# A DeepNorm decoder layer on one core: plain products for six contraction tiles of each down projection, the bias table in the mixer, memory queries by seven block products

## The chip, the core and the metric

One core of a Trainium2 chip runs the whole layer in one launch. The metric is the device time of that core in microseconds. Before the change three runs took 1260.83, 1260.99 and 1263.0 us (median 1260.99).

The engines named below: TensorE (PE in the rows) multiplies matrices and transposes, its weight loads are listed as PEld; VectorE (DVE), ScalarE (ACT) and GpSimd (POOL) work elementwise; SyncE (SP) and GpSimd issue DMAs.

## The reference

One layer for 512 tokens of width 1024, in four post-normalised parts:

```
h = LN1(alpha*h + 0.5*SwiGLU_1(h))            # w1, w3: 1024x2816, w2: 2816x1024
h = LN2(alpha*h + W_o[g_mla*Up_mla(MLA(h)) + g_diff*Up_diff(Diff(h))])
h = LN3(alpha*h + MemCrossAttn(h, mem))       # 4 heads of 256, 256 memory rows
h = LN4(alpha*h + 0.5*SwiGLU_2(h))
```

`SwiGLU(h) = (silu(h w1) * (h w3)) w2`. The mixer (second part) has eight latent-attention heads and four differential heads; the logits of the latter get a relative bias, looked up in a table of 32 buckets. The memory attention is `q = h w_q`, `k, v = mem w_kv`, softmax over the 256 memory rows, and an output projection `w_o`.

## The kernel before

All products keep close to full precision: each operand is split into a high and a low part in a rounded format, and a product is three matrix instructions, high x high, high x low and low x high (`mm3`). So every loaded weight tile [128, 1024] passes ScalarE or VectorE for the high part (a cast) and VectorE for the low part (a subtraction), and so does every activation tile.

**Seven products for eight.** Most of the feed-forward networks run by a scheme that multiplies 2x2 block matrices with seven block products, on sums and differences of the blocks. `products` (line 569) does it for a pair of hidden tiles: weight blocks come from a `Unit` (line 485), which loads four blocks of [128, 1024], adds some of them on VectorE and splits seven tiles; the sums of h are made once (`sums_of_h`, line 540) from the raw transposed h (`h_raw`). Each of the seven is 24 matrix instructions with 256 columns; results are combined on the way out. `down7` (line 722) does the same for four tiles of the hidden dimension in the down projection: seven products of 12 instructions with 512 columns, on sums of the gated activations (`Forms`, line 681).

**A feed-forward network** (`ffn`, line 639) has 22 hidden tiles. Tiles 0 and 1 are plain. Then come five groups: two calls of `seven`, two hidden tiles each, and one `down7` for four tiles (0 to 19 in all). Groups 0 to 3 add their results to an accumulator in DRAM by accumulating DMAs of GpSimd (after ScalarE has copied them from PSUM); group 4 adds on VectorE onto `res.acc`, which is loaded back at the start of that group's second `seven`. The last sum (`Residual.add`, line 454) takes tiles 20 and 21 plainly, by token tile (four of 128) and half of the columns: 6 matrix instructions of 512 columns for each, whose result VectorE adds. After the second half of a token tile its layer norm follows (`Norm`, line 392), then eight transposes, from which `hT`, the split transposed h, is written.

**The mixer** (line 1159) begins with four gate projections in two halves of 256 tokens (`project_halves`, line 343): the first half needs two normalised token tiles. The feed-forward network after the third norm begins in the same way.

**The table** (`bias_table`, line 811, with `lam_calc`, line 829) is made in the first network, from a mark at 200 us of the planner's clock: a 33-row one-hot matrix times the bias rows, two products in four passes, stored to DRAM; the differential heads read it later.

**Memory** (`memory`, line 1359): keys (8 weight tiles, no use of h), then the queries plainly, one projection of 24 instructions with 512 columns for each of 8 tiles, then values in two halves (48 instructions each). `mem_heads` (line 1289) runs beside this: for each pair of heads four score tiles, softmax, transposes, and the outputs; the second pair starts when the first pair's outputs are issued. The output projection adds in two steps of four contraction tiles, the second with norm 3.

**What sets the order.** A planner (`Issue`, line 52) runs all these as generators. Each has a rank, lower first; a generator may wait for a mark, a time on the planner's clock. Elementwise work is issued when the planner's clock reaches its start, weight splits with a delay. A scheduler behind it assigns buffers and may move instructions forward; each engine then executes its own list in order. Weights come through three raw and five split buffers (`Weights`, line 269): a tile is fetched when an earlier one is done. Most other tiles share 20 buffers of 4 KB per partition (`slot`).

Of the kernel before, what the change touches and what calls it, by code (L numbers as in the profile page):

```python
# [18 lines left out]
P = 128  # L19
# [175 lines left out]
def layer(ctx: ExitStack, tc: tile.TileContext, a: dict, out: bass.AP):  # L195
# [197 lines left out]
    class Norm:  # L393
# [223 lines left out]
    def plan_ffn(n, w1, w3, w2):  # L617
        for f in range(2):
            W.plan(f"w1_{n}_{f}", w1[f])
            W.plan(f"w3_{n}_{f}", w3[f])  # L620

        def up(p):
            return Unit(f"wp{n}_{p}", [[w[2 * p + i % 2][:, i // 2 * 512:i // 2 * 512 + 512] for w in (w1, w3)] for i in range(4)], ORDER)

        def down(g):
            rows = [w2[f * P:(f + 2) * P].rearrange("(f p) c -> p f c", p=P) for f in (4 * g, 4 * g + 2)]
            return Unit(f"wd{n}_{g}", [rows[i // 2][:, :, i % 2 * 512:i % 2 * 512 + 512] for i in range(4)], DOWN)

        units = []
        for g in range(5):  # L630
            units += [up(2 * g + 1), up(2 * g + 2), down(g)]
        for u, v in zip(units, units[1:]):
            u.after = v
        for u in units:
            u.plan()
        for f in (20, 21):
            W.plan(f"w2_{n}_{f}", w2[f * P:(f + 1) * P])

    def ffn(n, src, ready=None):
        res = Residual(n, src)  # L640
        gT, sums, raw = {}, {}, {}
# [24 lines left out]
        def seven(p, late=()):  # L666

            gated = raw[p] = slot(f"G{n}_{p}", F32)

            def out(c, half, ps, sign):  # L670
                dst = gated[:, c, 256 * half:256 * half + 256]
                act.activation(dst, ps[:, :256], AF.Silu, scale=sign)
                dve.scalar_tensor_tensor(dst, ps[:, 256:], 0.5 * sign, dst, op0=ALU.mult, op1=ALU.mult)
                if half and p == 10:
                    f = 2 * p + c
                    gT[f] = slot(f"g{n}_{f}")
                    split(gT[f][:, 0], gT[f][:, 1], gated[:, c])

            return products(f"wp{n}_{p}", sums, out, dict(late))
# [36 lines left out]
        def load_old():  # L716
            for h in range(2):
                for c in range(2):
                    t = old[h, c] = slot(f"old{n}_{h}_{c}", F32)
                    sp.dma_start(t, rows(src[256 * h:256 * h + 256, c * 512:c * 512 + 512]))  # L720

        def down7(g, forms):

            def product(pss, i, first):
# [5 lines left out]
                W.done(f"wd{n}_{g}_{i}")  # L730

            def add(pss, h, c, sign, new=False):
                if g == 4:
                    for t in range(2):
                        dst = res.acc[2 * h + t][:, c * 512:c * 512 + 512]
                        dve.tensor_tensor(dst, dst, pss[t], op=ALU.add if sign > 0 else ALU.subtract)
                elif g == 0 and new:
                    st = old.pop((h, c))
                    for t in range(2):
                        dve.scalar_tensor_tensor(st[:, t], st[:, t], ALPHA, pss[t], op0=ALU.mult, op1=ALU.add if sign > 0 else ALU.subtract)  # L740
                    sp.dma_start(rows(acc[h, c]), st)
                else:
                    st = slot(f"st{n}_{g}_{h}_{c}", F32)
                    for t in range(2):
                        act.activation(st[:, t], pss[t], AF.Copy, scale=sign)
                    pool.dma_start(rows(acc[h, c]), st, accum_op=ALU.add)

            x = [bank(f"dx{n}_{g}_{t}") for t in range(2)]
            product(x, 1, True)
# [45 lines left out]
                    sp.dma_start(res.acc[t][:, c * 512:c * 512 + 512], acc[t // 2, c][t % 2 * P:t % 2 * P + P])  # L795

        load_old()
        for g in range(5):
            yield from seven(2 * g + 1)
            forms = Forms(g)  # L800
            late = {3: lambda: forms.make(1), 2: lambda: forms.make(2), 4: lambda: forms.make(5)}
            if g == 4:
                late[1] = load_acc
            yield from seven(2 * g + 2, late)
            yield from down7(g, forms)
        yield from res.add(lambda i, t: hl_of(gT[20 + i], slice(t * P, (t + 1) * P)), [f"w2_{n}_{f}" for f in (20, 21)], False, True)


    bias_dram = dram.tile([8, 32 * REL], F32, name="bias_dram")
# [1 line left out]
    def bias_table():  # L811
        rel = const.tile([33, 8], F32, name="rel")
        nc.vector.memset(rel[32:33], NEG)
        sp.dma_start(rel[0:32], a["rel_bias"])
        hot = arena.tile([33, REL], F32, tag="slot", name="hot")
        sp.dma_start(hot, a["onehot"])
        rows = arena.tile([8, REL], F32, tag="slot", name="rows")
        for c in range(2):
            ps = bank(f"rel{c}")
            matmul(ps[:8, :320], rel, hot[:, c * 320:(c + 1) * 320], True, True)  # L820
            dve.tensor_scalar(rows[:, c * 320:(c + 1) * 320], ps[:8, :320], -1.0, None, op0=ALU.mult)
            drop(ps)
        sp.dma_start(bias_dram.rearrange("h (p m) -> h p m", p=32), rows.unsqueeze(1).broadcast_to([8, 32, REL]))


    neglam = const.tile([P, 1], F32, name="neglam")
    gd = const.tile([P, 1], F32, name="gd")

    def lam_calc():
        room = slot("lam", F32, [P, 1024])  # L830
# [328 lines left out]
    def mixer():  # L1159
# [104 lines left out]
    def out_proj(n, w, src, xT, sizes):  # L1264
        res = Residual(n, src)
        k0 = 0
        for m in sizes:
            if n == 3 and k0 + m == KT:
# [7 lines left out]
    def plan_mem():  # L1276
        for j in range(KT):
            W.plan(f"mem_wk{j}", a["mem_wk"][j])
        for j in range(KT):
            W.plan(f"mem_wq{j}", a["mem_w_q"][j])  # L1280
        for c in range(2):
            for q in range(4):
                W.plan(f"mem_wv{c}_{q}", a["mem_wv"][c][:, q * D:(q + 1) * D])
        for k in range(KT):
            W.plan(f"mem_w_o{k}", a["mem_w_o"][k * P:(k + 1) * P])

# [72 lines left out]
    def memory():  # L1359
        def mk(k, toks):  # L1360
            return hl_of(memT[k // 2], slice((k % 2) * 256 + toks.start, (k % 2) * 256 + toks.stop))

        kk, q, vv, oT = [], [], [[None, None], [None, None]], [None] * KT
        for j in range(KT):
            w = W.take(f"mem_wk{j}")
            if j % 2 == 0:
                ps = bank(f"mk{j}")
            dst = ps[:, (j % 2) * 256:(j % 2) * 256 + 256]
            for k in range(KT):
                mm3(dst, hl_of(w, slice(k * P, (k + 1) * P)), mk(k, slice(0, 256)), k == 0, k == KT - 1)  # L1370
            W.done(f"mem_wk{j}")
            if j % 2:
                kk.append(slot(f"mk{j}"))
                split(kk[-1][:, 0], kk[-1][:, 1], ps)
                drop(ps)
            yield
        for t in range(NT):
            yield h_ready[2, t]
        issue.spawn(mem_heads(kk, q, vv, oT), 1)
        for j in range(KT):  # L1380
            ps = yield from project(f"mq{j}", W.take(f"mem_wq{j}"))
            W.done(f"mem_wq{j}")
            t = slot(f"mq{j}")
            split(t[:, 0], t[:, 1], ps, scale=MEM_SCALE)
            drop(ps)
            q.append(t)
            if j % 4 == 3:
                issue.set(mem_q[j // 4], *q)
            yield
        for c in range(2):  # L1390
# [8 lines left out]
            for b in range(2):  # L1399
# [2 lines left out]
                drop(pss[b])  # L1402
                vv[c][b] = v
            issue.set(mem_v[c], *vv[c])
        yield mem_out
        yield from out_proj(3, "mem_w_o", h_dram[1], oT, (4, 4))


    def tables():
        mark = Mark()  # L1410
        mark.floor = 200000.0
        yield mark
        consts()
        bias_table()
        lam_calc()

    def main():
        first_loads()
# [97 lines left out]
```

## Time and profile before

| | before |
|---|---|
| median of three runs | 1260.99 us |
| profiled execution, its own time | 1261.45 us |
| its span, first to last instruction | 1259.70 us |
| mean granted TensorE clock | 0.988 |
| TensorE busy | 1214.5 us, 96% |
| VectorE busy | 1019.4 us, 81% |
| ScalarE busy | 551.0 us, 44% |

Busy time of TensorE contains the pipelined ends of its matrix instructions; the time that a group of them takes is read as the distance from its start to the start of the next. [...]

### The profile page before, as it was taken

To read this page: it belongs to the slowest core of one execution; us is meant where nothing else is said; L and a number is where in the kernel's file an instruction comes from. 1 tells how busy PE (TensorE), PEld (TensorE's weight loads), DVE (VectorE), ACT (ScalarE), POOL (GpSimd) and SP (SyncE) were. 2 spreads that over 40 slices of the span, in tenths; PEclk is the share of its full clock that TensorE was granted. 3 is DMA by queue.
4 is the path that set the end of the run, shared out by engine and by line. 5 is a ranking of instruction groups with operands and counts; after the bars stand their busy time and mean duration, and the time that the engine had idled before them with its cause. 6 is when DMAs were issued, how large, how long until landed. Compare 5 with 4: busy or idle time off the path is not lost. (4 is left out here: it accounts for less than half of the span.)

```text
span 1259.7 us, 19354 instructions
## 1 busy us (share of the span) xinstructions
PE 1214.5 (96%) x7530; PEld 1080.1 (86%) x7530; DVE 1019.4 (81%) x1590; ACT 551.0 (44%) x970; POOL 105.5 (8%) x101
## 2 busy tenths in 40 slices
PE   7999998999979999999999999999999999999995
PEld 5989897889869987877778889888899898999994
DVE  8999989789981799666665695555799999999998
ACT  5343635254432477434441244342453445445451
POOL 0001111111010000000000000000010102130300
PEclk9999999899979999999999999999999999999998
DMA  9749596869231321242233436244493667795941
GB/s 328 220 130 270 114 255 140 201 131 287 73 134 55 124 65 34 64 138 84 84 101 100 150 137 214 72 129 151 162 295 97 173 195 185 184 236 140 254 140 67
DMA packets 86591, 192.52 MB, mean 153 GB/s; under 512 B 7875, under 2 KB 9667, under 8 KB 86500
## 3 DMA queue, kind: packets, MB, share of 16 engines
q1 hardware_dynamic: 68004, 155.64, 37.1%
q0 software_dynamic: 18496, 35.66, 16.1%
q8 instruction: 59, 0.97, 0.3%
q14 instruction: 32, 0.26, 0.1%
HBM read 152.86 MB, written 38.40 MB: 152 GB/s over the span
## 5 line engine op out<-in xcount | busy, mean ns | idle before, releaser
L178 DVE TENSOR_TENSOR wp_hl<-wp_b,wp_hl 128x1024 fp32r<-128x1024 f32 x140 | 168.2, 1220 | 12.9 <-ACT wp_hl L178 10.6
L260 PE MATMUL pzwp<-S,wp_hl 128*128 128x256 f32 x960 | 124.2, 286 | 0.3 <-DVE S L178 0.3
L260 PE MATMUL pxwp<-S,wp_hl 128*128 128x256 f32 x960 | 122.6, 283 | 1.6 <-ACT p_wp L178 1.6
L260 PEld LDWEIGHTS pzwp<-S,wp_hl 128*128 128x128 f32 x960 | 120.0, 194 | 1.6 <-issue 1.1
L260 PE MATMUL pxwp<-hT,wp_hl 128*128 128x256 f32 x960 | 119.9, 281 | 1.3 <-ACT wp_hl L178 1.3
L260 PEld LDWEIGHTS pxwp<-hT,wp_hl 128*128 128x128 f32 x960 | 117.3, 188 | 4.2 <-ACT wp_hl L178 1.7
L260 PEld LDWEIGHTS pxwp<-S,wp_hl 128*128 128x128 f32 x960 | 118.3, 191 | 2.0 <-ACT p_wp L178 2.0
L178 ACT CAST wp_hl<-wp_b 128x1024 fp32r<-128x1024 f32 x75 | 78.7, 1051 | 93.3 <-PE pxwp L260 51.6
L260 PE MATMUL dx<-wd_hl,A 128*128 128x512 f32 x480 | 117.4, 391 | 1.6 <-DVE acc L178 1.2
L260 PEld LDWEIGHTS dx<-wd_hl,A 128*128 128x128 f32 x480 | 88.2, 188 | 21.2 <-issue 3.2
L178 DVE TENSOR_TENSOR wp_b<-wp_b,wp_b 128x1024 f32<-128x1024 f32 x80 | 97.4, 1219 | 0.6
L178 DVE TENSOR_TENSOR wd_hl<-wd_b,wd_hl 128x1024 fp32r<-128x1024 f32 x70 | 85.2, 1220 | 9.2 <-ACT wd_hl L178 9.2
L170 POOL DMA_DIRECT2D acc<-st x48 | 59.5, 1561 | 379.7 <-ACT st L178 205.1
L178 ACT CAST wd_hl<-wd_b 128x1024 fp32r<-128x1024 f32 x52 | 54.5, 1052 | 54.5 <-PE pxwp L260 24.9
L260 PE MATMUL pywp<-hT,wp_hl 128*128 128x256 f32 x480 | 60.6, 280 | 0.3 <-ACT wp_hl L178 0.3
L260 PE MATMUL dz<-wd_hl,A 128*128 128x512 f32 x240 | 59.2, 392 | 0.5 <-ACT st L178 0.3
L260 PEld LDWEIGHTS pywp<-hT,wp_hl 128*128 128x128 f32 x480 | 58.3, 188 | 0.5 <-ACT wp_hl L178 0.5
L260 PE MATMUL pw<-hT,w_hl 128*128 128x256 f32 (+1 forms) x288 | 49.8, 333 | 6.8 <-DVE w_hl L178 5.0
L260 PEld LDWEIGHTS dz<-wd_hl,A 128*128 128x128 f32 x240 | 44.5, 188 | 11.0 <-ACT st L178 1.1
L260 PEld LDWEIGHTS pw<-hT,w_hl 128*128 128x128 f32 x288 | 42.2, 194 | 13.5 <-ACT hT L178 7.2
L178 DVE CAST wp_hl<-wp_b 128x1024 fp32r<-128x1024 f32 x65 | 46.1, 710 | 7.4 <-PE pzwp L260 6.1
L260 PE MATMUL pgd<-hT,w_gd_hl 128*128 128x512 f32 x192 | 47.5, 400 | 0.0
(333 smaller groups left out, 2300.9 us busy)
## 6 DMA issues: line engine op xcount, KB each, us to landing
wp_b<-in_ffn_w SPq DMA_DIRECT2D x160, 256.0 KB, 6.9
wd_b<-in_ffn_w SPq DMA_DIRECT2D x50, 512.0 KB, 10.0
acc<-st POOLq DMA_DIRECT2D x48, 512.0 KB, 9.9
wd_b<-in_ffn_w POOLq DMA_DIRECT2D x20, 512.0 KB, 12.9
h_dram<-acc SPq DMA_DIRECT2D x12, 512.0 KB, 3.1
w_raw<-in_ffn_w SPq DMA_DIRECT2D x11, 512.0 KB, 5.3
w_gm_raw<-in_w_gate SPq DMA_DIRECT2D x8, 512.0 KB, 3.5
acc<-old SPq DMA_DIRECT2D x8, 512.0 KB, 3.7
```

The lines of the kernel that those rows point to most:

```text
L170: return (name, 1000.0, 4000.0, lambda: getattr(engine, op)(*args, **kw)), args[:1], list(args)
L178: return (name, ns, 1500.0 if name == "sync" else 0.0, lambda: getattr(engine, op)(*args, **kw)), outs, ins
L260: issue.pe(lambda: nc.tensor.matmul(ps, w, x, start=start, stop=stop, skip_group_check=again), ps, w, x)
```

## The change

Three parts.

1. Down projections: the fifth group keeps its two calls of `seven` but has no `down7`. Hidden tiles 16 and 17 go through a new plain `down` between the two calls, added to DRAM through `stage`; tiles 18 to 21 form the last sum, now four contraction tiles. `res.acc` is loaded during the sixth product of the last `seven`. The gated activations of tiles 20 and 21 are split by halves of the tokens as they come (`ends`).
2. The table is started as a generator of rank 8 in the mixer, when all four token tiles of norm 1 are transposed; it issues its loads, waits 15 us on the planner's clock, then does its products and the lambda computation (in a work tile).
3. Memory queries go through `Unit` and `products`, two blocks of four query tiles; the sums are made after norm 2 from copies of the raw transposed h. The first half of the values comes before the queries, the second half after them, and `mem_heads` starts after the queries.

```diff
@@ Norm.turn
-                if n == 3:
+                if n in (2, 3):
@@ plan_ffn
-        for g in range(5):
+        for g in range(4):
             units += [up(2 * g + 1), up(2 * g + 2), down(g)]
+        units += [up(9), up(10)]
...
             u.plan()
+            if u is units[-2]:
+                for f in (16, 17):
+                    W.plan(f"w2_{n}_{f}", w2[f * P:(f + 1) * P])
-        for f in (20, 21):
+        for f in range(18, 22):
@@ seven, out
-                if half and p == 10:
+                if p == 10:
+                    if half not in ends:
+                        ends[half] = slot(f"ge{n}_{half}").rearrange("p c (i t) -> p c i t", i=2)
+                    split(ends[half][:, c, 0], ends[half][:, c, 1], dst)
+                elif half and p > 7:
@@ ffn
+        def stage(pss, h, c, sign):
+            st = slot(f"st{n}_{h}_{c}", F32)
+            for t in range(2):
+                act.activation(st[:, t], pss[t], AF.Copy, scale=sign)
+            pool.dma_start(rows(acc[h, c]), st, accum_op=ALU.add)
+
+        def down(fs):
+            keys = [f"w2_{n}_{f}" for f in fs]
+            ws = [W.take(key) for key in keys]
+            for h in range(2):
+                for c in range(2):
+                    pss = [bank(f"ds{n}_{h}_{c}_{t}") for t in range(2)]
+                    for t in range(2):
+                        for w, f in zip(ws, fs):
+                            toks = slice((2 * h + t) * P, (2 * h + t + 1) * P)
+                            mm3(pss[t], hl_of(gT[f], toks), hl_of(w, slice(c * 512, c * 512 + 512)), f == fs[0], f == fs[-1])
...
+                    stage(pss, h, c, 1.0)
...
-        for g in range(5):
+        for g in range(4):
...
+        yield from seven(9)
+        yield from down(range(16, 18))
+        yield from seven(10, {2: load_acc})
+        fs = range(18, NF)
...
+        yield from res.add(part, [f"w2_{n}_{f}" for f in fs], False, True)
@@ bias_table
         sp.dma_start(hot, a["onehot"])
+        yield later(15000.0)
...
+        lam_calc()
@@ mixer
+        issue.spawn(bias_table(), 8, ready[NT - 1])
@@ plan_mem
+        values(0)
+        units = [Unit(f"mem_wq{u}", [[a["mem_w_q"][4 * u + 2 * w + i % 2][:, i // 2 * 512:i // 2 * 512 + 512] for w in range(2)]
+                                     for i in range(4)], ORDER) for u in range(2)]
+        units[0].after = units[1]
...
+        values(1)
@@ memory
+        issue.spawn(summing(), 0)
...
+        yield from values(0)
+        yield summed
+        for u in range(2):
+            def out(c, half, ps, sign, u=u):
+                for w in range(2):
+                    j = 4 * u + 2 * w + c
+                    if not half:
+                        q[j] = slot(f"mq{j}")
+                    toks = slice(256 * half, 256 * half + 256)
+                    split(q[j][:, 0, toks], q[j][:, 1, toks], ps[:, 256 * w:256 * w + 256], scale=sign * MEM_SCALE)
+            yield from products(f"mem_wq{u}", sums, out)
+        issue.spawn(mem_heads(kk, q, vv, oT), 1)
...
+        yield from values(1)
@@ tables
-        bias_table()
-        lam_calc()
```

## Rows read from the trace of the kernel before

**Rows 1.** The page, first part: busy us (share of the span), number of instructions.

```profile
PE 1214.5 (96%) x7530; PEld 1080.1 (86%) x7530; DVE 1019.4 (81%) x1590; ACT 551.0 (44%) x970; POOL 105.5 (8%) x101
```

**Rows 2.** Waits of TensorE: total us, times, longest us.

```profile
PE trh L269 <- DVE acc L178: 9.3, 2, 6.0
...
PE rel L260 <- DMA hot<-in_onehot: 4.4, 1, 4.4
```

**Rows 3.** Windows: stretch, busy us of each engine, clock, DMA share, GB/s.

```profile
364.00:368.00 4.00, 0.00 (x0) 0.00 (x0) 4.00 (x7) 1.80 (x4) 0.93 (x2) 0.50 0.27 63
...
220.00:224.00 4.00, 2.19 (x4) 0.36 (x4) 0.97 (x3) 0.20 (x1) 3.47 (x3) 0.50 0.54 76
```

**Rows 4.** Timeline, first network: start, duration, engine, operation, count, idle before.

```profile
152.96 3.02 PE L260 MATMUL pxwp<-hT,wp_hl 128*128 128x256 f32 x24
...
212.03 3.01 PE L260 MATMUL pxwp<-hT,wp_hl 128*128 128x256 f32 x24
...
215.51 0.37 SPq L178 DMA_DIRECT2D hot<-in_onehot  x1
...
221.81 2.30 PE L260 MATMUL rel<-hot,rel 33*8 33x320 f32 x4 [4.41 <-DMA hot<-in_onehot]
...
224.04 5.13 PE L260 MATMUL pzwp<-S,wp_hl 128*128 128x256 f32 x24
...
283.94 3.02 PE L260 MATMUL pxwp<-hT,wp_hl 128*128 128x256 f32 x24
```

**Rows 5.** Chain that ended last, last network: start, us to the next piece, what.

```profile
1116.69 2.85 PE pxwp L260 x24
...
1122.41 2.88 PE pxwp L260 x24
...
1175.75 2.85 PE pxwp L260 x24
```

**Rows 6.** Timeline at the third norm.

```profile
906.25 5.71 PE L260 MATMUL res_mem_w_o<-mem_w_o_hl,moT 128*128 128x512 f32 x24
...
912.58 7.29 PE L260 MATMUL pw<-hT,w_hl 128*128 128x256 f32 x60
```

**Rows 7.** Timeline at the end of the last network.

```profile
1238.18 9.23 PE L260 MATMUL res_w<-w_hl,g 128*128 128x512 f32 x40
...
1250.88 0.68 DVE L178 SCALAR_TENSOR_TENSOR acc<-acc,res_w 128x512 f32<-128x512 f32 x1
```

**Rows 8.** Timeline at the end of the first network.

```profile
359.23 3.68 PE L269 MATMUL trh<-ident,acc 128*128 128x128 f32 x16 [3.33 <-DVE acc L178]
...
372.13 22.77 PE L260 MATMUL pw_gm<-hT,w_gm_hl 128*128 128x256 f32 x192
...
394.74 9.53 PE L260 MATMUL cq<-w_cq_hl,hT 128*128 128x384 f32 x53
```

**Rows 9.** Groups by form, 773 to 867: count, busy us, mean ns, idle before.

```profile
L260 PE MATMUL mq<-hT,mem_wq_hl 128*128 128x512 f32 x192 | 46.1, 398 | 0.0
...
L178 DVE TENSOR_TENSOR mem_wq_hl<-mem_wq_raw,mem_wq_hl 128x1024 fp32r<-128x1024 f32 x5 | 6.1, 1226 | 12.7 <-ACT mem_wq_hl L178 12.7
```

**Rows 10.** Windows: before the queries, and blocks of the last network.

```profile
760.00:780.00 20.00, 20.00 (x141) 18.69 (x140) 11.34 (x12) 9.66 (x12) 0.00 (x0) 1.00 0.74 244
...
1060.00:1080.00 20.00, 20.00 (x170) 20.00 (x170) 17.01 (x20) 7.37 (x12) 6.23 (x5) 1.00 0.99 244
```

**Rows 11.** Timeline, scores and softmax of the first pair of heads.

```profile
798.52 5.92 PE L260 MATMUL mx<-mk,mq 128*128 128x256 f32 x48
...
804.29 0.50 ACT L178 ACTIVATE me<-me,mrs 128x256 f32<-128x256 f32 x1
...
805.92 0.52 ACT L178 ACTIVATE me<-me,mrs 128x256 f32<-128x256 f32 x1
...
807.48 0.51 ACT L178 ACTIVATE me<-me,mrs 128x256 f32<-128x256 f32 x1
```

**Rows 12.** The page, DMA issues: count, KB each, median us to landing.

```profile
wp_b<-in_ffn_w SPq DMA_DIRECT2D x160, 256.0 KB, 6.9
```

More of the change, by code (lines that the diff above doesn't have):

```diff
@@ L640, in ffn @@
         res = Residual(n, src)
-        gT, sums, raw = {}, {}, {}
+        gT, ends, sums, raw = {}, {}, {}, {}
         acc = {(h, c): dram.tile([256, 512], F32, name=f"acc{n}_{h}_{c}") for h in range(2) for c in range(2)}
@@ L720, in load_old @@
                     sp.dma_start(t, rows(src[256 * h:256 * h + 256, c * 512:c * 512 + 512]))
+        def stage(pss, h, c, sign):
[13 more added lines that the diff above has]
+                            mm3(pss[t], hl_of(gT[f], toks), hl_of(w, slice(c * 512, c * 512 + 512)), f == fs[0], f == fs[-1])
+                    if h and c:
+                        for key in keys:
+                            W.done(key)
+                    stage(pss, h, c, 1.0)
+                    drop(*pss)
+                    yield
         def down7(g, forms):
@@ L732, in add @@
             def add(pss, h, c, sign, new=False):
[L733 to L737, printed above, removed]
+                if g == 0 and new:
                     st = old.pop((h, c))
@@ L742, in add @@
                 else:
[L743 to L746, printed above, removed]
+                    stage(pss, h, c, sign)
             x = [bank(f"dx{n}_{g}_{t}") for t in range(2)]
@@ L797, in ffn, with part @@
         load_old()
-        for g in range(5):
+        for g in range(4):
             yield from seven(2 * g + 1)
             forms = Forms(g)
[L801 to L804, printed above, removed]
+            yield from seven(2 * g + 2, {3: lambda: forms.make(1), 2: lambda: forms.make(2), 4: lambda: forms.make(5)})
             yield from down7(g, forms)
-        yield from res.add(lambda i, t: hl_of(gT[20 + i], slice(t * P, (t + 1) * P)), [f"w2_{n}_{f}" for f in (20, 21)], False, True)
+        yield from seven(9)
+        yield from down(range(16, 18))
+        yield from seven(10, {2: load_acc})
+        fs = range(18, NF)
+        def part(i, t):
+            if i < 2:
+                return hl_of(gT[fs[i]], slice(t * P, (t + 1) * P))
+            return [ends[t // 2][:, i - 2, j, t % 2 * P:t % 2 * P + P] for j in (0, 1)]
+        yield from res.add(part, [f"w2_{n}_{f}" for f in fs], False, True)
     bias_dram = dram.tile([8, 32 * REL], F32, name="bias_dram")
@@ L823, in bias_table, with later @@
         sp.dma_start(bias_dram.rearrange("h (p m) -> h p m", p=32), rows.unsqueeze(1).broadcast_to([8, 32, REL]))
+        lam_calc()
+        yield
+    def later(ns):
+        mark = Mark()
+        mark.floor = issue.clock + ns
+        return mark
     neglam = const.tile([P, 1], F32, name="neglam")
@@ L829, in lam_calc @@
     def lam_calc():
-        room = slot("lam", F32, [P, 1024])
+        room = wk("lam")
         lam = room[:, :256].rearrange("p (a b) -> p a b", a=4)
@@ L1267, in out_proj @@
         for m in sizes:
-            if n == 3 and k0 + m == KT:
+            if k0 + m == KT:
                 h_raw.extend(slot(f"hraw{j}", F32) for j in range(4))
@@ L1278, in plan_mem, with values @@
             W.plan(f"mem_wk{j}", a["mem_wk"][j])
-        for j in range(KT):
-            W.plan(f"mem_wq{j}", a["mem_w_q"][j])
-        for c in range(2):
+        def values(c):
             for q in range(4):
                 W.plan(f"mem_wv{c}_{q}", a["mem_wv"][c][:, q * D:(q + 1) * D])
+        values(0)
+        units = [Unit(f"mem_wq{u}", [[a["mem_w_q"][4 * u + 2 * w + i % 2][:, i // 2 * 512:i // 2 * 512 + 512] for w in range(2)]
+                                     for i in range(4)], ORDER) for u in range(2)]
+        units[0].after = units[1]
+        for u in units:
+            u.plan()
+        values(1)
         for k in range(KT):
@@ L1361, in mk, with summing, values @@
             return hl_of(memT[k // 2], slice((k % 2) * 256 + toks.start, (k % 2) * 256 + toks.stop))
[L1363 to L1390, printed above, removed]
+        kk, q, vv, oT = [], [None] * KT, [[None, None], [None, None]], [None] * KT
+        sums, summed = {}, Mark()
+        def summing():
+            for t in range(NT):
+                yield h_ready[2, t]
+            mark = sums_of_h(2, sums)
+            summed.floor, summed.ops = mark.floor, mark.ops
+        def values(c):
             pss = [bank(f"mv{c}_{b}") for b in range(2)]
@@ L1404, in memory @@
             issue.set(mem_v[c], *vv[c])
+        issue.spawn(summing(), 0)
+        for j in range(KT):
+            w = W.take(f"mem_wk{j}")
+            if j % 2 == 0:
+                ps = bank(f"mk{j}")
+            dst = ps[:, (j % 2) * 256:(j % 2) * 256 + 256]
+            for k in range(KT):
+                mm3(dst, hl_of(w, slice(k * P, (k + 1) * P)), mk(k, slice(0, 256)), k == 0, k == KT - 1)
+            W.done(f"mem_wk{j}")
+            if j % 2:
+                kk.append(slot(f"mk{j}"))
+                split(kk[-1][:, 0], kk[-1][:, 1], ps)
+                drop(ps)
+            yield
+        yield from values(0)
[10 more added lines that the diff above has]
+        issue.spawn(mem_heads(kk, q, vv, oT), 1)
+        for hp in range(2):
+            issue.set(mem_q[hp], *q)
+        yield from values(1)
         yield mem_out
@@ L1409, in tables @@
     def tables():
-        mark = Mark()
-        mark.floor = 200000.0
-        yield mark
+        yield later(200000.0)
         consts()
-        bias_table()
-        lam_calc()
     def main():
```

## The prediction

> **What bounds the kernel now.** The page's first part comes first: TensorE is busy for 96% of the span and VectorE for 81% [rows 1]. So a stage costs what TensorE executes in it, plus the places where it stands still. Those are listed by the view of waits: 9.3 us in two waits for the layer norm that ends the first feed-forward network, and 4.4 us in one wait for the table of buckets [rows 2]. [...] The timeline then gives the length of each stage as the distance between the starts of like products. The last view is the end of the span, where TensorE has finished 12 us before the kernel.
>
> The sum is made against the profiled execution: 1261.45 us, of which the span is 1259.70 and 1.75 lies around it. The median of the runs is 0.46 lower.
>
> **The bias table leaves the first network.** A group of four contraction tiles (two blocks of seven products up, one down) takes 59.07 us where nothing disturbs it (152.96 to 212.03) and 71.91 us where the table is built (212.03 to 283.94) [rows 4]. The load of the one-hot matrix was issued at 215.51; TensorE stood for 4.4 us until 221.81 [rows 2, 4], ran the table's four passes in 2.3 us at half clock, and its next 24 products took 5.1 us [rows 4] where 24 take 2.88 [rows 5]. The group's excess is 12.84 us; I take all of it as the table's, since the same group in the last network takes 59.06 (1116.69 to 1175.75) [rows 5]. What comes back in the mixer is the four passes: at full clock half of 2.3, so 1.15 us. The load is issued in the mixer too, with 15 us planned between its issue and the products; it needed 6.3 us here (215.51 to 221.81) [rows 4] and stays hidden. The small lambda computation goes with it and takes a work tile: its multiplication stands in VectorE's queue behind a DMA, and behind it stand the mixer's weight splits. If that load is late, w_cq and w_ckv splits are late with it; VectorE has slack there, so I take nothing, with a bound of 6 us. Bounds of this part: -13 and -4. Taken: -11.7.
>
> **End of the first network.** Removed: a down block of 7 x 12 = 84 products of 512 columns and a last sum of 48. Added: a plain down part for tiles 16 and 17 of 48, and a last sum of 96. That is 12 more. The third norm's last sum has the new form: from 906.25 to 912.58 lie 24 products and the eight transposes of a token tile [rows 6]. The old last sum runs 40 in 9.23 [rows 7], so 0.231 each and 5.54 for 24, which leaves 0.79 for the transposes; 12 products cost 2.8 us. What VectorE loses is more: seven weight splits become four, and the sums of activations, their seven splits and the 14 additions from PSUM go; ScalarE and four accumulating DMAs take over the adds of tiles 16 and 17. The DMAs have the whole of the next block (seven products of 2.88 us [rows 5]) to land before the accumulators are read back.
>
> Before, the last sum offered 12 products (2.8 us) per token tile, and VectorE's norm fell behind: matmuls ended at 355.9, transposes began at 359.23, the gates at 372.13 [rows 8]. Now there are 24 per tile, 5.5 us. The third norm has exactly that form (24 products per token tile, then projections by halves that need the first two tiles only), and there the projections follow the last products with eight transposes between them and no gap [rows 6]. I take that row as the model. The old stretch from 283.94 to the end of the gates at 394.74 [rows 4, 8] is 110.8 us. The new one is 14 products of seven-product blocks (40.3), 48 plain (11.1), 96 (22.2), four transposed tiles (3.2) and 192 gate products (394.74 - 372.13 = 22.6): 99.4, and 0.3 for small waits. Against cover: four of the five split-weight buffers now hold down tiles until the last products, so three of the four gate weights are split only afterwards, while the fourth gives TensorE 3 us. Bounds: -12 (no waits at all) and -4 (those splits exposed). Taken: -11.1.
>
> **End of the last network.** Before, from the last group's start at 1175.75 [rows 5] to the span's end are 83.95 us. TensorE's last product ended at 1247.41, and the last token tile's sum reached VectorE only at 1250.88, since VectorE was behind [rows 7]. From there to the end are 8.8 us of pure chain (sums, square, power, two scalings, store); without the previous tile's scalings in between it is some 0.5 us shorter. New: 40.3 + 11.1 + 22.2 = 73.6 to the last product, then 8.5. That is 82.1, so -1.8. Bounds: -3 and +2.8 (only the added products count).
>
> **Memory queries.** Before: 192 products of 512 columns, 46.1 us busy including the last's end [rows 9], so about 45.0 to the next. After: 14 products of 2.88 us [rows 5] = 40.3: -4.7. Keys, values, scores and outputs are the same work, only moved. Two things stand against this.
>
> First, VectorE. It must make the sums of h (16 operations of about 0.6 us), the four value splits of the first half and the first query splits, two with an added block sum, all before and just after the block products start. Before, it was 11.3 us busy of 20 in that stretch [rows 10], five query weight splits of 1.23 among it [rows 9]: about 5 remain. To these come 9.7 of sums, 6.3 for values, 5.7 for three query tiles and 2 of casts, some 29 us where 24 lie between the norm's end and the block products. A block costs VectorE 17.0 us of 20 in the last network [rows 10], and here 2 more for splitting the queries, so a backlog is not won back soon. I take 3 us of waiting (bounds 0 and 8).
>
> Second, cover. Before, the scores and softmax of the first pair of heads had 24 us of query products beside them. Now both pairs have only the second half of the values, 11 us in four steps, of which the first pair takes all. From the first pair's scores before: scores start at 798.52, the second token tile's softmax is finished at 804.8, the third's at 806.4, the fourth's at 808.0 [rows 11]. So with nothing beside them the last three transposes can start 6.3, 7.9 and 9.5 us after the scores' start, and the outputs, after two casts and two subtractions, at about 11.5, where TensorE has 5.75 us of scores and 1.6 of transposes to do. So it waits 4.2 us, in pieces of up to 1.6. I take 4 (bounds 0 and 8, the latter with a fallen clock). Total for this part: -4.7 + 3 + 4 = +2.3, bounds -4.7 and +11.
>
> Before this, ScalarE copies the second norm's transposes (16 of 0.3 us): it does the same at the third norm, where TensorE did not wait [rows 6], so nothing is added.
>
> **Sum.** 1261.45 - 11.7 - 11.1 - 1.8 + 2.3 = 1239.2; less the 0.46 to the median, 1238.7.
>
> **The rivals.**
> 1. The table's wait moves with the table. For: the wait is for a DMA, and queue and one-hot load go along. Against: the 15 us. If the products still come before the data, the mixer pays 4.4 us and the half clock (about 2), and the lambda load delays the w_cq splits by some 2: first part -3 instead of -11.7, so 1247. Chance 0.09.
> 2. The first network's end stays exposed because the gate weights wait for buffers. For: four of five are held. Against: the third norm [rows 6], where also four tiles are held. Second part -4: 1246. Chance 0.11.
> 3. The second pair's softmax lies open and the clock falls. For: 3.3 us of idle time after 355.9 were followed by 0.50 [rows 3, 8]. Then the 24 output products (5.5 us) run at half clock for a good part, and VectorE's backlog takes its upper bound: +8 to +10 on the third part, so 1248. Chance 0.12.
> [...]
> 4. Slower than before: the buffer pool is too small. Keys, memory, values, sums, queries and two sets of four weight blocks count up to 28 tiles for 20 buffers. If the second set of blocks can be loaded only when the first is fully used, each of the two blocks of products waits for a 6.9 us load [rows 12], an addition and a split (about 11 us), with 3 us of half clock behind it, and the following value loads wait in the same queue: 28 us or more on the third part. 1267. It decides from 24 us of waits on. Against: the first set is free after its sixth split, before the first queries need buffers, and my count then stays at 20. Chance 0.06.
>
> **How the numbers follow.** Forecast 1238.7, chance 0.60, with a range of its own of 1232 to 1246: below, the memory part without waits; above, its bounds. Rivals 1 to 3 end from 1246 to 1248, rival 4 at 1267; 0.02 is left. 1231 to 1250 leaves out rival 4, two rivals together and little else. A difference under 0.2% (2.5 us) cannot be told from none. Faster: forecast and rivals 1 to 3, less pairs that add up, 0.91; same 0.02; slower 0.07.
>
> **What would show it.** The group from 212 us on takes 59 to 60 us and the clock is 1.00 there. After the first norm, gate products follow within 1 us of the transposes and the windows read 1.00. The last product ends about 8.5 us before the span's end. Two blocks of queries take 40 to 44 us; between the second pair's scores and outputs TensorE idles some 4 us. I am wrong if the mixer shows a wait for the one-hot load or for w_cq or w_gm splits of over 2 us, if query block loads are issued only after earlier products, or if the clock falls in the memory stage.

## The result, and the profile after

The changed kernel takes 1245.07 us (median of 4 runs, 1242.51 to 1245.68) beside 1261.74 for the kernel before (1260.83 to 1263.0): ratio 0.9863, 95% interval 0.9846 to 0.9881. It is 16.7 us faster; the forecast was 1238.7. The profiled execution took 1245.68, so profile against profile the gain is 15.8 us where the sum gave 22.3.

The stages are read as in the prediction, by the starts of like products on TensorE's timeline. Each entry is a length in us.

| stage | before | predicted | after |
|---|---|---|---|
| start to the compressed queries (cq): first network, its end, gate products | 394.7 | 370.8 | 371.6 |
| cq to the first scores | 52.3 | 53.5 (the table's products) | 57.0 |
| first scores to the first value products (vd) | 55.4 | 55.4 | 59.5 |
| rest of the mixer, keys of the memory block | 270.7 | 270.7 | 270.9 |
| memory: values, queries, scores, outputs | 93.0 | 95.3 | 94.8 |
| output projection | 46.4 | 46.4 | 46.1 |
| last network, to its last product | 334.8 | 336.8 | 336.2 |
| from there to the end | 12.3 | 8.5 | 7.8 |

The two networks and the memory block came out within 1.5 us of the forecast. The whole miss lies in the second and third lines, where the mixer lost 8.8 us instead of 1.2.

The page's first line and TensorE's waits after (total us, times, longest us). Against [rows 1, 2] the waits for the norm and for the one-hot load are gone, and at the places of [rows 3] the clock is 1.00 (220 to 224 and, at the new end of the first network, 344 to 356); a wait for the mixer's qT is new, and so are the small ones of the memory block.

```profile
PE 1214.3 (98%) x7698; PEld 1088.4 (87%) x7698; DVE 1029.4 (83%) x1620; ACT 544.4 (44%) x986; POOL 110.7 (9%) x105
...
PE sm L260 <- ACT qT L178: 1.9, 1, 1.9
...
PE pxmem_wq L260 <- ACT p_mem_wq L178: 1.2, 1, 1.2
PE trx L269 <- ACT me L178: 1.1, 1, 1.1
```

The first network's timeline after (start, us, engine, operation, count) answers to [rows 4, 8]: the group of four tiles from 213.38 to 272.45 takes 59.07 us, and the gates follow the third token tile's transposes at once.

```profile
213.38 3.02 PE L260 MATMUL pxwp<-hT,wp_hl 128*128 128x256 f32 x24
...
272.45 3.02 PE L260 MATMUL pxwp<-hT,wp_hl 128*128 128x256 f32 x24
...
347.31 1.04 PE L269 MATMUL trh<-ident,acc 128*128 128x128 f32 x8
348.11 10.10 PE L260 MATMUL pw_gm<-hT,w_gm_hl 128*128 128x256 f32 x84
...
371.60 0.69 PE L260 MATMUL cq<-w_cq_hl,hT 128*128 128x384 f32 x3
```

**Where the mixer's time went.** SyncE's queue after: the table is stored at 381.95, and behind the store stand the mixer's weight loads. The second number is the time that SyncE spent in issuing.

```profile
381.95 0.81 SPq L178 DMA_DIRECT2D bias_dram<-rows  x1
388.68 0.34 SPq L178 DMA_DIRECT2D w_gm_raw<-in_w_gate  x1
389.58 4.20 SPq L178 DMA_DIRECT2D w_kn_raw<-in_w_kn  x1
393.87 1.99 SPq L178 DMA_DIRECT2D w_qr_raw<-in_w_qr  x1
395.91 0.43 SPq L178 DMA_DIRECT2D cs<-in_rope  x1
```

Before, w_kn was issued in 0.33 us and landed after 4.5; now 4.20 and 11.0. The first line below is from before, the second its landing (KB, median us), the third the landing after:

```profile
411.61 0.33 SPq L178 DMA_DIRECT2D w_kn_raw<-in_w_kn  x1
...
w_kn_raw<-in_w_kn SPq DMA_DIRECT2D x1, 512.0 KB, 4.5
...
w_kn_raw<-in_w_kn SPq DMA_DIRECT2D x1, 512.0 KB, 11.0
```

While the store runs the DMA engines move 47 GB/s, at a busy share of 0.45 (382 to 390, the last two numbers):

```profile
382.00:390.00 8.00, 8.00 (x47) 8.00 (x46) 3.03 (x5) 2.30 (x5) 0.94 (x2) 1.00 0.45 47
```

The store reads 640 KB from only 8 partitions (`rows` is 8 x 640); `e5` below stores the same bytes from 128.

The scores' start and the clock after it, after (windows: busy us of each engine, clock, DMA share, GB/s):

```profile
428.62 4.02 PE L260 MATMUL sm<-kT,qT 96*128 96x512 f32 x14 [1.94 <-ACT qT L178]
```

```profile
424.00:428.00 4.00, 2.67 (x12) 1.85 (x10) 3.94 (x7) 2.02 (x5) 0.00 (x0) 1.00 0.59 153
428.00:432.00 4.00, 3.38 (x13) 2.91 (x14) 3.84 (x8) 1.80 (x3) 0.00 (x0) 0.70 0.11 44
432.00:436.00 4.00, 4.00 (x14) 3.52 (x13) 3.58 (x11) 1.31 (x4) 0.00 (x0) 0.50 0.32 94
```

The splits come late. Before, w_qr, w_kn and w_v were cast ahead of the latents' second transposes (first fence); after, w_qr and w_v are cast behind a gate's activation, right before their products (second fence).

```profile
424.58 0.53 ACT L178 CAST w_qr_hl<-w_qr_raw 128x384 fp32r<-128x384 f32 x1
...
425.93 0.62 ACT L178 CAST w_v_hl<-w_v_raw 128x512 fp32r<-128x512 f32 x1 [0.83 <-PE ckv L260]
...
429.42 1.04 PE L269 MATMUL trc<-ident,cn 128*128 128x128 f32 x8
```

```profile
411.10 0.69 ACT L178 ACTIVATE gm<-pgm,half_b 128x512 f32<-128x512 f32 x1 [1.98 <-PE pgm L260]
...
411.68 0.51 ACT L178 CAST w_qr_hl<-w_qr_raw 128x384 fp32r<-128x384 f32 x1
...
412.08 0.62 ACT L178 CAST w_v_hl<-w_v_raw 128x512 fp32r<-128x512 f32 x1
...
412.30 2.42 PE L260 MATMUL qr<-cT,w_qr_hl 128*128 128x512 f32 x9
```

These two casts did not wait for their loads: w_qr had landed by 401.1 and w_v by 409.3. They stand late in ScalarE's list, which is fixed before the kernel runs. So in this kernel TensorE waits for the order of the splits, not for a load itself; that the list changes with the store's shape is seen in `e5` below, and why it does is not shown. From 424 to 428 VectorE is busy 3.94 of 4 us and TensorE runs short of work; from 432 to 436 the clock is at half.

### The profile page after: what moved, and what is told of

Read it like the earlier page. It is cut to its first block, busy times and chain, and to the rows that moved or that the text cites. A ratio compares the mean times of both kernels' runs of the same rounds, so it can differ in the third digit from the quotient of the medians.

```text
span 1243.9 us, 19733 instructions
## 1 busy us (share of the span) xinstructions
PE 1214.3 (98%) x7698; PEld 1088.4 (87%) x7698; DVE 1029.4 (83%) x1620; ACT 544.4 (44%) x986; POOL 110.7 (9%) x105
## 4 chain that ended last, share of the span: by engine, by line
PE 81%; DVE 11%; DMA 3%; issue 2%; ACT 2%; SPq 0%; POOL 0%; DVEq 0%; POOLq 0%; ACTq 0%
PE pxwp L260 18%; PE pzwp L260 9%; PE dx L260 7%; PE pywp L260 4%; PE res_w L260 3%; PE pgd L260 3%; PE res_mem_w_o L260 3%; PE res_w_o L260 3%; PE dz L260 3%; PE pw L260 2%; PE vd L260 2%; PE qd L260 2%; PE pw_gm L260 2%; PE kd L260 2%; PE ds L260 2%
## 5 line engine op out<-in xcount | busy, mean ns | idle before, releaser
L170 POOL DMA_DIRECT2D acc<-st x56 | 69.5, 1555 | 426.7 <-ACT st L178 228.8
L178 ACT CAST wp_hl<-wp_b 128x1024 fp32r<-128x1024 f32 x69 | 72.0, 1052 | 77.4 <-PE pxwp L260 41.6
L260 PE MATMUL dx<-wd_hl,A 128*128 128x512 f32 x384 | 93.2, 391 | 0.3 <-DVE old L178 0.3
L260 PEld LDWEIGHTS dx<-wd_hl,A 128*128 128x128 f32 x384 | 70.7, 188 | 14.9 <-issue 1.1
L178 DVE TENSOR_TENSOR wd_hl<-wd_b,wd_hl 128x1024 fp32r<-128x1024 f32 x56 | 68.4, 1221 | 8.2 <-ACT wd_hl L178 8.0
L178 ACT CAST wd_hl<-wd_b 128x1024 fp32r<-128x1024 f32 x42 | 44.2, 1052 | 43.6 <-PE pxwp L260 21.9
L178 DVE CAST wp_hl<-wp_b 128x1024 fp32r<-128x1024 f32 x71 | 49.9, 704 | 8.8 <-PE ds L260 3.9
L260 PEld LDWEIGHTS pw<-hT,w_hl 128*128 128x128 f32 x288 | 43.3, 198 | 13.7 <-ACT hT L178 7.5
L260 PE MATMUL dz<-wd_hl,A 128*128 128x512 f32 x192 | 46.7, 390 | 0.0
L260 PE MATMUL res_mem_w_o<-mem_w_o_hl,moT 128*128 128x512 f32 x192 | 44.9, 392 | 0.0
```

Source lines behind the costliest of these rows:

```text
L170: return (name, 1000.0, 4000.0, lambda: getattr(engine, op)(*args, **kw)), args[:1], list(args)
L178: return (name, ns, 1500.0 if name == "sync" else 0.0, lambda: getattr(engine, op)(*args, **kw)), outs, ins
L260: issue.pe(lambda: nc.tensor.matmul(ps, w, x, start=start, stop=stop, skip_group_check=again), ps, w, x)
```

## The experiments

Theory: the table's presence in the mixer costs 6 to 7 us there through its store. Rival: the store is harmless and another part (the query blocks, the ends of the networks) fell short. Ratios and differences are against the kernel before, timed alongside (medians 1261.5 to 1262.0 us).

**Each part alone.** `e1` is the kernel before with the moved table, `e3` with the new ends of the networks, `e4` with the new memory block, `e2` the changed kernel with the table back in the first network, `e11` the changed kernel with the old memory block.

> Only the table and the lambda computation move into the mixer; down projections and memory queries as before. Theory (the store of the table, which reads 8 partitions, stands in SyncE's queue ahead of the attention's weight loads; their splits come late and TensorE's clock falls): the group from 212 us on loses 12.8 us, the mixer gets back 1.2 for the products and about 7.6 for waits and half clock, so 4 us faster than before. Rival (the mixer's loss belongs to the new end of the first network): 11.7 us faster, the mixer unchanged but for 1.2.

Measured: 1255.11 us, ratio 0.9948 (0.9935 to 0.9960), -6.4. The stages give both sides: cq starts at 383.0, 11.8 earlier (expected 12.8), and the mixer takes 4.2 more, not 8.8. Here two w_gm loads stand behind the store; the first lands after 13.5 us and TensorE waits 2.0 us for their splits, but w_kn is issued at 399.83 and lands after 4.8. So what the store costs depends on the loads that stand behind it, and with the new ends of the networks it costs more (`e11` below).

> The changed kernel with the table and the lambda computation back in the first network, as before the change; the other two parts stay. Theory: the first network's group takes 72 us again, the mixer 308 us as before; net 4 us slower than the changed kernel, 12 to 13 us faster than before. Rival (mixer's loss not from the table): 11.7 us slower than the changed kernel, so 5 us faster than before.

```
-        issue.spawn(bias_table(), 8, ready[NT - 1])
...
         consts()
+        bias_table()
+        lam_calc()
```

Measured: 1244.4, 0.9862 (0.9849 to 0.9876): the same as the changed kernel, which neither side expected: with the other two parts in, moving the table gained nothing. The mixer is whole again (52.3 and 55.5), but cq starts at 378.1, so the table costs 6.5 us in its old place. In this order the one-hot load is covered: TensorE's four passes start at 223.57 without a wait and take 1.24 us. The rest are waits for operands that VectorE and ScalarE deliver late, 4.4 us in all from 212 to 280.

> Only the down projections change. Theory: the end of the first network gives 11.6 us and the end of the last 3.1, so 14.7 us faster than before (1246.5), mixer unchanged. Rival (the mixer pays for the new end): 7 us faster.

Measured: 1251.38, 0.9918 (0.9904 to 0.9931), -10.2. The last network's end gains 2.9 in the trace, the first only 7.4, because the group in which the table is built takes 76.5 us (211.96 to 288.50) instead of 71.9 [rows 4]. In its trace TensorE's waits of that group, 212 to 290:

```profile
PE rel L260 <- DMA hot<-in_onehot: 4.0, 1, 4.0
PE dx L260 <- DVE A L178: 2.5, 2, 1.6
PE pxwp L260 <- ACT p_wp L178: 1.6, 1, 1.6
```

The second is new: VectorE splits the activations A late. What the table takes depends on the order around it, and that order moves with edits elsewhere: `e2` has the same code for the first network and differs only in the memory block, yet its group takes 67.1 us (212.00 to 279.12). So the parts do not add up: parts 1 and 2 gain 6.4 and 10.2 alone and 19.9 together (`e11`), parts 2 and 3 gain 10.2 and lose 2.9 alone and gain 17.1 together (`e2`).

> Only the memory queries go through seven block products. Theory: 4.7 us less of products against about 6 of waits: 1 to 2 us slower than before (1262.5). Rival: the waits seen in the changed kernel come from the other parts and the products' 4.7 us show: 1256.5.

Measured: 1264.44, 1.0023 (1.0014 to 1.0031), +2.9: this part alone costs time. The trace does not show where: the profiled execution, at 1262.25 the fastest of eleven, has 93.0 us for the memory block as before. The slowest, 1266.88, has a mean granted clock of 0.985, the profiled one 0.989.

> The changed kernel with its memory block as before: parts 1 and 2 alone. The prediction gave the block products a cost of 2.3 us, so it expects about 1242.8 us, 2 us below the changed kernel; by the run of that part alone, which cost 2.9 us, 1242 us. Rival: in the changed kernel the part is a gain that other losses hide, and without it the run takes 1246 us or more.

Measured: 1242.01, 0.9845 (0.9832 to 0.9859). Without the block products the kernel is 3.1 us faster, as the forecast said. The two profiles put only 1.6 us of it in the memory block and its projection (140.9 against 139.4). Another 2.4 lie ahead of them: this run has the changed kernel's mixer, with the same wait, yet there the clock stayed at 1.00:

```profile
424.00:428.00 4.00, 2.74 (x12) 1.88 (x10) 3.94 (x7) 2.03 (x4) 0.00 (x0) 1.00 0.51 142
428.00:432.00 4.00, 3.26 (x16) 2.57 (x17) 3.84 (x8) 1.85 (x3) 0.00 (x0) 1.00 0.13 54
432.00:436.00 4.00, 4.00 (x20) 3.40 (x20) 3.94 (x14) 1.63 (x5) 0.00 (x0) 1.00 0.30 94
```

Scores to values took 57.1 us here against 59.5: 2.4 us of the profile of the changed kernel are the fallen clock, which an execution may or may not meet.

**The store by itself.** `e5` spreads it over 128 partitions: each head's column of the table is repeated 16 times ahead of the products.

```
+        dve.tensor_copy(wide.rearrange("p (h r) -> p h r", r=16), rel.unsqueeze(2).broadcast_to([33, 8, 16]))
+        rows = arena.tile([P, REL], F32, tag="slot", name="rows")
...
+            matmul(ps[:, :320], wide, hot[:, c * 320:(c + 1) * 320], True, True)
...
-        sp.dma_start(bias_dram.rearrange("h (p m) -> h p m", p=32), rows.unsqueeze(1).broadcast_to([8, 32, REL]))
+        sp.dma_start(bias_dram.rearrange("h (r q m) -> (h r) q m", r=16, q=2), rows.unsqueeze(1).broadcast_to([P, 2, REL]))
```

> The changed kernel, but the table's product is made for 128 partitions (16 copies of each head's row), so its store of 640 KB reads 128 partitions with 2 pieces each instead of 8 with 32. Table, place and lambda computation stay. Theory (the store is what delays the weight loads): the store is done in 2 to 4 us, the attention's splits precede the gate activation again, the mixer loses only 1.2 us: 6 to 8 us faster than the changed kernel, 1237 to 1239. Rival (the products or the lambda computation at this place cost the 7.6 us): as the changed kernel, 1245.

Measured: 1238.95, 0.9810 (0.9797 to 0.9824), 6 us under the changed kernel. The stages are 53.8 and 56.2 us, 110.0 together; with the narrow store they are 114.1 at clock 1.00 (`e11`) and 116.5 with the fallen clock (the changed kernel), so the store's shape is worth 4.1 us and the clock behind it 2.4 more. w_qr is cast at 403.43, ahead of the second transposes again. SyncE's queue and the DMA issues (count, KB each, median us to landing) in its trace:

```profile
382.58 0.61 SPq L178 DMA_DIRECT2D bias_dram<-rows  x1
389.29 0.34 SPq L178 DMA_DIRECT2D w_gm_raw<-in_w_gate  x1
390.20 0.33 SPq L178 DMA_DIRECT2D w_kn_raw<-in_w_kn  x1
```

```profile
bias_dram<-rows SPq DMA_DIRECT2D x1, 640.0 KB, 3.4
w_gm_raw<-in_w_gate SPq DMA_DIRECT2D x1, 512.0 KB, 3.9
w_kn_raw<-in_w_kn SPq DMA_DIRECT2D x1, 512.0 KB, 4.8
```

The same bytes leave in 3.4 us, and the loads behind them are nearly as quick as before. Place, products and lambda computation stay, so the cause is the store from 8 partitions, not the table's work, except for the last 1 us (the mixer still loses 2.2 us where the products take 1.2).

`e6` leaves the store narrow but makes table and store 60 us later (`later(75000.0)`).

> The changed kernel with 75 us instead of 15 on the planner's clock between the table's load and its products, so that products, store and lambda computation come during the latent attention, when the weights of it are loaded. Theory: the mixer's start is free of it, 5 to 8 us faster than the changed kernel. Rival (products and lambda cost where they stand): 0 to 3 us faster, since VectorE is busier there.

Measured: 1239.23, 0.9822 (0.9809 to 0.9836). The store is issued at 444.47. The loads behind it, of w_vd, are issued in 0.34 us each, at 446.97 and 457.87 (in the changed kernel two of them stand 11 us apart as well), and no engine waits for a load from 430 to 500. From the scores to the values the run takes 57.3 us, the table's products among it.

`e9` issues the narrow store from another queue (`pool.dma_start` for `sp.dma_start`).

> The store of the bias table still reads 8 partitions, but POOL's queue issues it in place of SP's. If the mixer's loads were late because they stand behind the store in SP's queue, they are free of it: w_kn issues in 0.3 us and lands in about 4.5 us, w_qr and w_v likewise, the stretch from the compressed queries to the scores takes about 54 us (it took 57.0) and the run about 1239 us, as with the store spread over 128 partitions. Rival: the store holds the 16 DMA engines themselves for its 13 us, whichever queue issues it; then the loads still land in 7 to 11 us, the stretch takes 56 to 57 us and the run about 1245 us.

The narrow store is issued at 380.57 from GpSimd. SyncE's loads behind it, and the landings:

```profile
388.18 3.75 SPq L178 DMA_DIRECT2D w_kn_raw<-in_w_kn  x1
392.04 2.33 SPq L178 DMA_DIRECT2D w_qr_raw<-in_w_qr  x1
```

```profile
bias_dram<-rows POOLq DMA_DIRECT2D x1, 640.0 KB, 15.0
w_gm_raw<-in_w_gate SPq DMA_DIRECT2D x1, 512.0 KB, 10.8
w_kn_raw<-in_w_kn SPq DMA_DIRECT2D x1, 512.0 KB, 10.9
```

Measured: 1242.95, 0.9852 (0.9838 to 0.9865); cq to scores 57.5 us; the run lies between the two sides, 2.1 us under the changed kernel. My side of it failed: with the store out of their queue the loads are as slow. So a store issued by GpSimd slows SyncE's loads as well; through what is not shown. The DMA engines' busy share while the store ran was 0.45 in the changed kernel and 0.49 here (384 to 388). This trace has the direct link from a late load to TensorE that the changed kernel lacks: VectorE stands 7.92 us for w_gm, behind it in its list stands a step of the latents' norm, and TensorE's transposes wait for that.

```profile
397.94 0.69 DVE L178 CAST w_gm_hl<-w_gm_raw 128x1024 fp32r<-128x1024 f32 x1 [7.92 <-DMA w_gm_raw<-in_w_gate]
...
401.32 0.65 PE L269 MATMUL trc<-ident,cn 128*128 128x128 f32 x4 [2.48 <-ACT cn L178]
```

**The table early, without blocking.** `e7` runs table and lambda in the first network with the 15 us between load and products (`issue.spawn(bias_table(), 8)` behind `consts()`); `e10` does so too, but leaves the lambda in the mixer.

> The changed kernel with the table started in the first network as before the change, but with 15 us between load and products. Theory (two costs: the wait for the load, removed by the 15 us, and the slow store, which here stands ahead of the network's weight loads): the network's group is 1 to 5 us longer than 59.1, the mixer is as before: 3 to 7 us faster than the changed kernel. Rival (the wait for the load was all the cost in the first network): 7.6 us faster.

Measured: 1243.51, 0.9856 (0.9843 to 0.9870); cq starts at 378.1. That is 1.6 us under the changed kernel, less than either side expected and within the spread of the runs.

> The table runs early, in the first network, as in the run before of that kind, but the lambda stays in the mixer. The store is the narrow one, in the same place. If the first network's 6.5 us over the changed kernel came from the extra work of VectorE and ScalarE there (four small lambda operations, the exponential's two table loads of 1.28 us, which push the splits of the down products' operands back), most of it goes: the compressed queries start at about 373 us instead of 378, the mixer keeps 52.5 us, and the run takes 1238 to 1240 us. Rival: the narrow store delays the network's weight loads; then the lambda's absence changes nothing there: 377 to 378 us, and a run of about 1243 us.

Measured: 1243.11, 0.9854 (0.9841 to 0.9868); cq starts at 378.2, so the lambda was not it. TensorE's waits of e10 from 212 to 290 are all for splits of A:

```profile
PE dy L260 <- ACT A L178: 1.7, 1, 1.7
PE dy L260 <- DVE A L178: 1.7, 1, 1.7
```

None is for a load, and the loads of these down products were issued by 230, before the store at 245.10, so the narrow store did not delay them. The clock fell to 0.75 and 0.83 from 260 to 268, where ten products that took 2.4 us before the change took 4.0. What is left is the table's own work and the changed order of VectorE's and ScalarE's lists; no run tells these apart, so this stays open.

**The second pair's softmax.** `e8` lets the output projection start when the first pair of heads is done, so that its first products (those that need only these heads) stand beside the second pair's softmax.

```
-        yield mem_out
+        yield mem_first
...
+            if n == 3 and k0:
+                yield mem_out
```

> The changed kernel, but the first half of the memory's output projection starts when the first pair of heads has its outputs, so that it stands beside the second pair's softmax. Theory (TensorE waits there for want of work, and its clock falls): 4 to 5 us faster than the changed kernel. Rival (the gap is replaced by another wait, for accumulators or buffers): 0 to 1 us faster.

Measured: 1241.52, 0.9839 (0.9826 to 0.9852), 3.5 us less than the changed kernel. Memory block and projection together take 136.3 us instead of 140.9. The same place in the changed kernel, and then in `e8`:

```profile
843.12 0.66 PE L269 MATMUL trx<-ident,me 128*128 128x128 f32 x4 [0.61 <-DVE me L178]
844.84 1.49 PE L269 MATMUL trx<-ident,me 128*128 128x128 f32 x8 [1.07 <-ACT me L178]
846.79 2.07 PE L260 MATMUL mo<-ptx,mv 128*128 128x512 f32 x4 [0.46 <-ACT ptx L178]
```

```profile
841.72 3.01 PE L260 MATMUL res_mem_w_o<-mem_w_o_hl,moT 128*128 128x512 f32 x12
844.56 0.60 PE L269 MATMUL trx<-ident,me 128*128 128x128 f32 x4
844.92 3.00 PE L260 MATMUL res_mem_w_o<-mem_w_o_hl,moT 128*128 128x512 f32 x12
```

The gaps in brackets are filled, and the clock, 0.75 and 0.82 in the changed kernel from 844 to 852, is 1.00 there. Part of that is the execution: `e2`, `e4`, `e6` and `e10` have the same three waits and kept 1.00 (the four output products behind them took 1.20 us in `e4`, `e6` and `e10`; the mean clock of `e2` was 0.999), while `e5`, `e7` and `e9` fell as the changed kernel did (1.83 to 2.08 us for the four). Block and projection took 138.9 us in `e10`, which waits 0.7 us less at the block products; so some 1.4 of the 4.6 us are an estimate for the clock, and 2.1 are the waits in brackets.

**Both mends.** `e12` is `e5` and `e8` in one.

> Both mends in one: the bias table stored from 128 partitions (6 us when alone) and the output projection's first products set beside the second pair's softmax (3.5 us when alone). They act in stages 350 us apart, so they should add: about 1235 us. Rival: the second eats part of the first, since both leave less of VectorE idle: 1238 us or more.

Measured: 1234.27 (1233.30 to 1235.37), 0.9785 (0.9772 to 0.9798). It beats both kernels, and the mends add, with a little over: 6.1 and 3.5 alone, 10.8 together. Whether the wide store with the old memory block would do as well was not run.

## Why the prediction was right or wrong

- **Direction and range:** right. The sum was 6.5 us too hopeful in the profiled execution. That the time stayed in the range is partly luck: the miss lies in a term of the first part, whose bound of 6 us it passed, and the range's upper end came from the memory part's bounds.
- **The table leaves the first network (-12.8 there):** right. The group took 59.07 us, and `e1` gained 11.8 to cq; the changed kernel's first groups started 1.35 us later than before, which is why cq comes 0.8 later than forecast.
- **"VectorE has slack there, so I take nothing, with a bound of 6 us":** this is the step that failed. I asked whether the lambda's load would be late and counted the table's products, but the step also moved the store, and I never priced it. In the new place 1.7 MB of loads follow it within 14 us (w_gm, w_kn, w_qr and the rotary table) and are needed soon after. Measured: 7.6 us beyond the products, of which 2.4 are the clock of that execution; `e5` and `e6` get 6 us back. The store had not been free in its old place either: five loads for the down products, right behind it there, landed after 19.4 us before the change (median; 7.5 in the changed kernel, where the store stands elsewhere). How much of the 12.84 us was the store's is not measured.
- **End of the first network (99.4 + 0.3):** right. It took 99.15 (272.45 to 371.60). The third norm was the model, and as there no gap opened; the cover that I feared for, the split-weight buffers, was not short: TensorE has no listed wait from 272 to 372.
- **End of the last network (-1.8):** right in kind, a little small: -3.1. The last product ended 7.8 us before the span's end, not 8.5.
- **Memory queries (+2.3):** right in size for the medians (`e4` +2.9, `e11` 3.1) and for the changed kernel's trace (+1.8), but it is no fixed cost. With the projection the same block took from 138.9 (`e10`) to 142.6 us (`e9`) in eight profiles, where the old one took 139.4 in each of four; the longer ones are those where the clock fell or TensorE waited longer at the block products. The two blocks took 42.3 us (forecast 43.3), with 1.8 us of waits for VectorE and ScalarE. The open softmax cost 2.1 us in waits and, in the changed kernel's profile, an estimated 1.4 in clock, where I had priced 4; `e8` gets 4.6 back.
- **Rival 1 (the table's wait moves with the table, 1247):** right in place and nearly in size, wrong in mechanism: TensorE never waited for the one-hot load. `e5`, where table and products stay and only the store's shape changes, shows that the store carried most of the cost.
- **Rivals 2 and 4:** did not occur. **Rival 3:** the clock did fall behind the second pair's softmax, but only to 0.75 and 0.82 over 8 us, not for 8 to 10 us of loss. I had no mixed stretch of gaps and short products to judge by; there are eight now, with the same waits of 0.6, 1.1 and 0.5 us, and the clock fell in four of them and stayed at 1.00 in four; what decides between the two is not shown.
- **What would make it wrong:** I listed TensorE's waits of over 2 us in the mixer. The largest was 1.9; the cost lay in many smaller ones, in a slower order and in the clock, which a threshold on single waits does not see. One listed sign did come: the clock fell in the memory stage (844 to 852).

## What to carry to other kernels

When a step is moved, list every DMA that it issues, with the number of partitions that each reads or writes, and ask which loads come next in the new place: here a store from 8 partitions slowed the loads issued while it ran (10.7 to 11.0 us to landing instead of 3.9 and 4.8), from SyncE's queue as from GpSimd's. Where the order of every engine's list is planned anew at each edit, gains of parts need not add; time each alone and each undone. Compare the granted clock of two profiles stage by stage before you put a difference down to an edit. Where softmax lies open behind the last matmuls of a stage, the next stage's products that need only finished heads are the cover.

## What the runs showed of the hardware

- A store of 640 KB from 8 partitions took 15.0 us to land (`e9`), from 128 partitions 3.4 (`e5`). Loads of 512 KB to 128 partitions issued while the narrow one ran landed after 10.7 to 11.0 us in the changed kernel and `e9`, instead of 3.9 and 4.8 in `e5`. The first of them was issued in 0.33 to 0.34 us, the second in 4.20 and 3.75.
- The same instructions with the same 1.9 us wait ran at clock 1.00 in one execution (`e11`) and at 0.70, then 0.50 in another (the changed kernel); in `e8` it was 0.54, then 0.61. It is worth 2.4 us, where the changed kernel's runs spread over 3.2 (1242.5 to 1245.7).
